# A two-layer hybrid trunk on one core: first modulation by quarters, constants on a second queue, shorter roots, and weights of the second layer split ahead

## The chip, the core and the metric

The kernel runs on one core of a Trainium2 chip. Its engines are TensorE (PE; its weight loads are listed apart as PEld), VectorE (DVE), ScalarE (ACT), GpSimd (POOL) and SyncE (SP), which issues transfers to 16 shared DMA engines. The metric is the device time of one execution in microseconds. The kernel before takes 1523.9 us (median of three runs, 1523.51 to 1525.08).

## What is computed

One inference step over 640 tokens of 1024 features: 128 prompt tokens and 512 latent tokens. Layer 0 has a mixer of gated linear attention and retention heads, layer 1 multi-head latent attention. Each layer ends in a squared-ReLU MLP with 4096 hidden features. Every sub-layer has a root-mean-square norm before and after it, and shift, scale and gate from a conditioning vector:

```python
def rms_norm(x, g=None):
    xf = x.astype(jnp.float32)
    y = xf * lax.rsqrt(jnp.mean(jnp.square(xf), axis=-1, keepdims=True) + EPS)
...
def ada_mod(cond, w_ada, b_ada):
    m = jnp.einsum('bd,de->be', jax.nn.silu(cond), w_ada) + b_ada
    return jnp.split(m[:, None, :], 6, axis=-1)

def pre_norm_mod(x, g, shift, scale):
    return rms_norm(x, g) * (1.0 + scale) + shift

def post_norm_residual(x, y, g, gate):
    return x + gate * rms_norm(y, g)

def sq_relu_mlp(h, w1, w2):
    u = jax.nn.relu(jnp.einsum('bld,df->blf', h, w1))
    return jnp.einsum('blf,fd->bld', jnp.square(u), w2)
```

The result must have float32 precision.

## The kernel before

**Tiling and precision.** The tokens are five tiles of 128 (`NT = 5`, tile 0 the prompt). A float32 product is made of three: each operand is split into a high part (`wh`, a cast by ACT) and a low part (`wl`, a difference by DVE), and `mm3` (382) multiplies high by high, low by high and high by low. `wp` is a tile that holds both parts of a narrow weight. `hT` holds the turned, modulated activations, high and low.

**Order of the work.** The program is written as generators. A list scheduler (`Weave`, 95 to 258) runs them when the program is built, with a cost table (`way`, 267) that says how long each instruction should take, and so fixes one instruction order for each engine. `_issue` (210) holds the rule for a transfer: an issue of 0.47 us, then its bytes on a modelled DMA resource. All transfers are issued by SP. A thread with a smaller priority number goes first. Rooms are `Slots`: `raw` (3) for weights as loaded, `wp` (10) for split weights, `tmp` (4), `rows` (4), and PSUM banks as `psg` (3) and `psum` (5). `weights` (478) goes through one list of weight pieces in order, takes a `raw` slot and loads; `weight_rooms` (495) takes the room for the split parts; `weight_split` (525) casts and subtracts. As one instruction is recorded from one place, every row of the profile has the line L269, and tiles tell the groups apart.

**Head.** `main` (960) loads the conditioning vectors (`cc`), `ident`, then biases and norm gains (`vec`, `post`) and `fold`. `e<-cc` on ACT starts the SiLU; `wide` holds its transpose as a stationary operand. `ada_first` (755) makes shift and scale of layer 0 by halves of 512 columns from `rada` tiles (w_ada); `FIRST_LOADS` (2312) is the order of the first loads: a for a rada load of 512 KB, x for a token tile, w for the start of the weights, c for the constants. `ada_four` (623) runs four matmuls, `ada_turned` (629) copies the row and folds it into columns. `pre_norm` (806) squares, takes the inverse root (`rsqrt`, 388), scales `x` into `xn`, turns it (`ps<-ident,xn`), makes `h` from it with shift and scale (first half all on DVE, second half all on ACT), and casts `hT`. `gemm_first` (573) multiplies it with the first 480 columns of w_in_even (`pg<-wh,hT`), half by half. `make_tables` (1496) loads the tables of the even layer late, after all first loads.

**Tails.** `out_proj` (1044) and `mlp` (1094) each have a `tail` per tile: square with a running sum (`junk,sm`), gate, `residual` (857) with an inverse root, and the next `pre_norm`. In an MLP's tail the scaled `x` is `y`. `plan` (910) lists the weight pieces: `ODD_GROUPS` are the 256 query columns and then 320 others of w_in_odd, four pieces each. The odd layer (`odd`, 1885) gives its three `psg` banks to `psum` right after the rotary query products (2042); `norm256` (1954) has one more root.

Of the kernel before, what the change touches and what calls it, by code (L numbers as in the profile page):

```python
# [94 lines left out]
class Weave:  # L95
# [114 lines left out]
    def _issue(self, eng, start):  # L210
# [13 lines left out]
        if port:  # L224
            start = max(start, self.clk.get("port", 0.0))
            self.clk["port"] = start + us
        if eng == "SP":
            th.issue = self.clk[eng] = start + 0.47
            self.clk["DMA"] = max(self.clk.get("DMA", 0.0), th.issue + 1.1) + us
            end = self.clk["DMA"] + 1.0  # L230
            th.end = end if not beside else max(th.end, end)
            if not beside:
                th.time, th.eng = max(th.time, end), eng
        else:
            self.clk[eng] = th.time = start + us
            th.eng = eng
# [24 lines left out]
class Engine:  # L261
# [5 lines left out]
    def way(self, fn, a, k):  # L267
# [6 lines left out]
        if fn == "dma_start":  # L274
            return "SP", out.shape[0] * n * 4 / 350e3, emit, False
# [56 lines left out]
class Trunk:  # L332
# [68 lines left out]


# [75 lines left out]
    def weights(self):  # L478
# [16 lines left out]
    def weight_rooms(self, loads):  # L495
        for item, load in zip(self.wlist, loads):
            if isinstance(item, Event):
                yield item
                continue
# [24 lines left out]

    def weight_split(self, raw, hr, hi, lo, held, ev, eng):
# [12 lines left out]
    def nat_units(self, w, groups, lo="vector", pair=False, rooms=[None] * 4, prio=1):  # L538
# [9 lines left out]
        return [[self.weight(src(cols, k0), [2, sum(n for _, n in cols)], lo, pair, None, rooms[k0 // 2], prio)  # L548
# [24 lines left out]
    def gemm_first(self, units, n, out, ready):  # L573

        banks = []
        for half in range(2):
            us = []
            for t in range(NT):
                yield ready[t][half]
                if half == 0:  # L580
                    banks.append((yield from self.take(self.psg, [P, 512], F32, "pg")))
                ps, hp = banks[t]
                for i in range(2):
                    if t == 0:
                        us.append((yield units[half * 2 + i]))
                    wh, wl, held = us[i]
                    for k in range(2):
                        kc = half * 4 + i * 2 + k
                        self.mm3(ps[:, :n], self.hT[0][:, t, kc], self.hT[1][:, t, kc], wh[:, k], wl[:, k],
                                 kc == 0, kc == KC - 1)  # L590
                    if t == NT - 1:
                        self.drop(*held)
                    yield
                if half:
                    self.w.set(out[t], banks[t])
# [27 lines left out]
    def ada_four(self, ps, rows, start, stop):  # L623

        self.nc.tensor.batch("matmul", [
            ((ps[32 * j:32 * j + 32], self.wide[:, kc, 2 - 2 * sec:34 - 2 * sec], raw), dict(start=start, stop=stop))
            for j, (raw, kc, sec) in enumerate(rows)], 1.4)

    def ada_turned(self, ps, n, row):

        nc = self.nc
        nc.scalar.copy(row, ps)
        yield
        for j in range(4):
# [120 lines left out]
    def ada_first(self, mod, halves, prepared, x_go, c_go):  # L755
# [5 lines left out]
        nc.vector.memset(self.wide, 0.0)  # L761

        def load():
            parts = iter([(0, sec, half, k0) for half in range(2) for k0 in range(0, KC, 2) for sec in (1, 0)])
            xs = iter(x_go)
            for kind in FIRST_LOADS:
# [4 lines left out]
                elif kind == "c":  # L771
                    w.set(c_go)
                else:
                    yield from self.ada_loads([next(parts)], self.wp, 2)
# [6 lines left out]
        for half in range(2):  # L781
            ps, hp = yield from self.bank()
            row, hw = yield from self.take(self.tmp, [P, 512], F32, "row")
            todo = [(k0, sec) for k0 in (0, 4) for sec in (1, 0)]

            for i, (k0, sec) in enumerate(todo):
                got, held = [], []
                for kc in range(k0, k0 + 4):
                    raw, hr = yield self.ada_ev[0, sec, half][kc]
                    got.append((raw, kc, sec))  # L790
                    held += hr
                self.ada_four(ps, got, i == 0, i == 3)
                self.drop(*held)
                yield
            yield self.cols_ready
            yield from self.ada_turned(ps, 4, row)
            pv = ps[:, 0:16].rearrange("p (j s c) -> p s c j", s=2, c=2)
            for sec in range(2):
                self.mod_cols(0, sec, res[sec][:, :, half * 4:half * 4 + 4], half * 4, pv[:, sec])
                w.set(halves[half][sec], res[sec])  # L800
                if half:
# [4 lines left out]
    def pre_norm(self, t, x, xn, sm, mods, ready, halves=None):  # L806
# [11 lines left out]
        evs = [Event(), Event()]  # L818

        def rest(half):  # L820
            shift, scale = halves[half] if halves else mods
            if half or not halves:
# [3 lines left out]
            for j in range(4):  # L826
                kc = half * 4 + j
# [3 lines left out]
            h, hh = yield from self.take(self.tmp, [P, 4, P], F32, "h")  # L831
            for j in range(4):
                kc = half * 4 + j
                src, bias, gain = ps[:, j * P:(j + 1) * P], sh[:, c, kc:kc + 1], sc[:, c, kc:kc + 1]
                if half:
# [5 lines left out]
            k = slice(half * 4, half * 4 + 4)  # L841
# [4 lines left out]
            w.set(evs[half])  # L846
            if halves:
                w.set(ready[t][half])

        w.spawn(rest(0))  # L850
        w.spawn(rest(1))
        yield evs[0]
        yield evs[1]
        if not halves:
            w.set(ready[t])

    def residual(self, x, yg, sm, dst=None):

        nc = self.nc
        nc.vector.tensor_scalar(sm[:, 6:7], sm[:, 4:5], sm[:, 5:6], D * EPS, op0=ALU.add, op1=ALU.add)  # L860
        yield
        yield from self.rsqrt(sm[:, 6:7], sm[:, 7:8], sm[:, 3:4], 1.0 / D)
# [19 lines left out]
    def run(self):  # L882
# [17 lines left out]
        self.ident = const("ident", [P, P])  # L900
        self.fold, self.wide = const("fold", [P, P]), const("wide", [P, KC, 34])
# [8 lines left out]
    def plan(self):  # L910
# [11 lines left out]
        self.u_in_odd = (self.nat_units(io["w_in_odd"][0], ODD_GROUPS[:1], pair=True)  # L922
                         + self.nat_units(io["w_in_odd"][0], ODD_GROUPS[1:], rooms=self.odd_rooms))
# [36 lines left out]
    def main(self):  # L960
# [7 lines left out]
        prepared, self.cols_ready = Event(), Event()  # L968
        c_go, x_go = Event(), [Event() for _ in range(NT)]
        halves = [[Event(), Event()] for _ in range(2)]  # L970
# [4 lines left out]
        ready = [[Event(), Event()] for _ in range(NT)]  # L975

        def first(t):
# [4 lines left out]
            yield from self.pre_norm(t, x, xn, sm, None, ready, halves)  # L982
            self.drop(hx, hy, hs)

        for t in range(NT):
            w.spawn(first(t), 0.0)

        load = lambda dst, src: lambda: nc.sync.dma_start(dst, src)
        k_rows = lambda nm: io[nm].rearrange("l (k p) -> (l k) p", p=P)
        arrived, arrived2 = Event(), Event()  # L990
        w.aside(load(cc[0:8], io["c_ctx"].rearrange("(k p) -> k p", p=P)),
                load(cc[8:16], io["c"].rearrange("b (k p) -> (b k) p", p=P)),
                load(self.ident, io["consts"][:, C_ID:C_ID + P]), then=lambda at: w.set(arrived, None, at))
        w.spawn(self.ada_first(mod, halves, prepared, x_go, c_go), 1.4)
        yield c_go
        w.aside(load(vec[0:96], k_rows("b_ada")), load(vec[96:112], k_rows("norm_mix_pre")),
                load(vec[112:128], k_rows("norm_mlp_pre")), load(post[0:16], k_rows("norm_mix_post")),
                load(post[16:32], k_rows("norm_mlp_post")),
                load(self.fold, io["consts"][:, C_FOLD:C_FOLD + P]), then=lambda at: w.set(arrived2, None, at))
        yield arrived  # L1000
        nc.scalar.activation(e[0:16], cc[0:16], AF.Exp, scale=-1.0)
        nc.vector.tensor_scalar(e[0:16], e[0:16], 1.0, None, op0=ALU.add)
        nc.vector.reciprocal(e[0:16], e[0:16])
        nc.vector.tensor_mul(cc[0:16], cc[0:16], e[0:16])
        ps, hp = yield from self.bank()
        nc.tensor.transpose(ps[:, 0:16], cc[0:16], self.ident[0:16, 0:16])
        nc.vector.tensor_copy(self.cT, ps[:, 0:16])
        w.set(prepared)
        yield arrived2
        yield 1.0  # L1010
        nc.tensor.transpose(ps[:, 128:256], vec, self.ident)
        nc.tensor.transpose(ps[:, 256:288], post[0:32], self.ident[0:32, 0:32])
        nc.vector.tensor_copy(self.cols, ps[:, 128:288])
        self.drop(hp, hc, he, hv, ho)
        w.set(self.cols_ready)
# [28 lines left out]
    def out_proj(self, units, oready, gate, mods, parked, gfree):  # L1044
# [6 lines left out]
        def tail(t):  # L1051
# [4 lines left out]
            for half in range(2):  # L1056
                ps, hp = yield out[half][t]
                s = slice(half * 512, half * 512 + 512)
                nc.scalar.activation(self.junk[:, 0:512], ps, AF.Square, accum_out=sm[:, 4 + half:5 + half])
                nc.vector.tensor_mul(y[:, s], ps, gr[c][:, s])  # L1060
                self.drop(hp)
# [1301 lines left out]
```

## Time and profile before

| | us |
|---|---|
| median of the runs | 1523.9 |
| the profiled execution | 1522.98 |
| its span | 1521.2 |
| PE busy | 1473.8 (97%) |
| DVE busy | 1092.6 (72%) |
| ACT busy | 651.7 (43%) |
| mean granted PE clock | 0.987 of full speed |

In the page PE's matmuls are listed apart from its weight loads, and matmuls overlap, so that a group's busy time divided by its count is the pace in a row of many and the mean of one is longer. A row of a timeline has start, duration, engine, operation, tiles and count; a bracket at its end tells how long the engine was idle before and what ended that. SPq is SP issuing. With PE at 97% the places to look at are those few in which it is not busy: the windows below give these.

### The profile page before, as it was taken

Reading aid. Unit: us, or ns where it says so; the run is one execution under the profiler, and the core shown is the slowest. Engines: PE = TensorE matmul, PEld = TensorE weight load, DVE = VectorE, ACT = ScalarE, POOL = GpSimd, SP = SyncE. Lnnn points to the kernel's source line nnn. Section 1 sums busy time; section 2 is a strip of 40 time slices with the busy share of each in tenths; the row PEclk is TensorE's granted clock in tenths of the full one; section 3 lists DMA queues with packets and bytes.
Section 4 is the critical chain, followed back from the end, with each engine's and each line's share of the span. In section 5 each row is a group of like instructions: output and inputs, shape, how many; then the busy total and the mean of one; then the engine's idle time right before and its main releaser. Section 6 shows DMA issues by size and latency. Waiting matters only on the chain.

```text
span 1521.2 us, 22996 instructions
## 1 busy us (share of the span) xinstructions
PE 1473.8 (97%) x8587; PEld 1308.4 (86%) x8587; DVE 1092.6 (72%) x2247; ACT 651.7 (43%) x1526; POOL 113.0 (7%) x133
## 2 busy tenths in 40 slices
PE   5999999999999999999997999999999999999997
PEld 2688888889899899899896989997889989988996
DVE  4464674757767877777868788885765869996776
ACT  3583533646433232233246366673654323332332
POOL 0000200101021021021010100000002000000000
PEclk8999999999999999999998999999999999999999
DMA  9546222133555444445414110104422223432332
GB/s 331 166 156 209 87 69 80 44 110 112 163 163 152 143 128 146 144 129 152 123 42 140 48 29 22 43 29 139 167 83 70 63 77 112 130 120 84 98 103 105
DMA packets 148176, 171.44 MB, mean 113 GB/s; under 512 B 12144, under 2 KB 92640, under 8 KB 148064
## 3 DMA queue, kind: packets, MB, share of 16 engines
q1 hardware_dynamic: 148064, 169.97, 36.4%
q8 instruction: 67, 1.10, 0.3%
q14 instruction: 45, 0.37, 0.1%
HBM read 161.36 MB, written 8.59 MB: 112 GB/s over the span
## 4 chain that ended last, share of the span: by engine, by line
PE 89%; DVE 4%; ACT 3%; DMA 2%; issue 1%; SPq 0%; DVEq 0%; ACTq 0%
PE p L269 55%; PE pg L269 19%; PE ps L269 13%; PE pqk L269 2%; DVE y L269 1%; PE pv L269 1%; ACT junk L269 1%; DVE sm L269 1%; DMA raw<-in_w_in_even 1%; DVE x L269 1%; DMA x<-in_x_sample 1%; DMA raw<-in_w_out_odd 1%; ACT h L269 0%; SPq L269 0%; DVE rope L269 0%
## 5 line engine op out<-in xcount | busy, mean ns | idle before, releaser
L269 PE MATMUL p<-wh,hid 128*128 128x512 f32 x1280 | 399.6, 391 | 0.0
L269 PEld LDWEIGHTS p<-wh,hid 128*128 128x128 f32 x1280 | 240.3, 188 | 49.3
L269 PE MATMUL p<-hT,wh 128*128 128x256 f32 (+1 forms) x1280 | 280.1, 310 | 0.0
L269 PE MATMUL pg<-wh,hT 128*128 128x512 f32 (+3 forms) x840 | 264.8, 389 | 0.0
L269 PE MATMUL p<-wl,hid 128*128 128x512 f32 x640 | 249.7, 390 | 0.0
L269 DVE TENSOR_TENSOR wl<-raw,wh 128x1024 fp32r<-128x1024 f32 (+3 forms) x141 | 167.9, 1195 | 73.8 <-ACT wh L269 73.4
L269 PEld LDWEIGHTS p<-hT,wh 128*128 128x128 f32 x1280 | 216.1, 190 | 0.8
L269 ACT CAST wh<-raw 128x1024 fp32r<-128x1024 f32 (+3 forms) x145 | 147.6, 1022 | 137.9 <-PE p L269 98.6
L269 PE MATMUL p<-hT,wl 128*128 128x256 f32 (+1 forms) x640 | 198.7, 310 | 0.0
L269 PEld LDWEIGHTS pg<-wh,hT 128*128 128x128 f32 x840 | 155.2, 190 | 32.3 <-issue 9.2
L269 DVE SCALAR_TENSOR_TENSOR ada<-rada,cT,ada 128x512 f32<-128x512 f32 x196 | 146.7, 778 | 0.0
L269 PE MATMUL pg<-wl,hT 128*128 128x512 f32 (+3 forms) x360 | 141.9, 394 | 0.0
L269 PEld LDWEIGHTS p<-wl,hid 128*128 128x128 f32 x640 | 120.3, 188 | 24.1
L269 DVE TENSOR_TENSOR y<-y,p 128x512 f32<-128x512 f32 x140 | 96.0, 686 | 58.1 <-PE p L269 57.3
L269 POOL TENSOR_TENSOR r<-r 128x384 f32<-128x384 f32 (+1 forms) x80 | 80.6, 1007 | 729.1 <-ACT hid L269 392.8
L269 PEld LDWEIGHTS p<-hT,wl 128*128 128x128 f32 x640 | 121.3, 190 | 0.0
L269 ACT ACTIVATE r<-p 128x384 f32<-128x384 f32 (+1 forms) x80 | 35.0, 438 | 157.1 <-PE p L269 157.1
L269 PE MATMUL p<-hT,wq 128*128 128x320 f32 x576 | 88.1, 310 | 0.0
L269 PEld LDWEIGHTS p<-hT,wq 128*128 128x128 f32 x576 | 85.5, 188 | 0.5
L269 PEld LDWEIGHTS pg<-wl,hT 128*128 128x128 f32 x360 | 68.7, 191 | 11.9 <-issue 2.5
L269 DVE TENSOR_TENSOR hid<-r,hid 128x384 fp32r<-128x384 f32 (+1 forms) x80 | 38.9, 487 | 46.4 <-POOL r L269 46.3
L269 ACT CAST wq<-tw 128x512 fp32r<-128x512 f32 x48 | 27.6, 618 | 71.0 <-DVE tw L269 61.7
(282 smaller groups left out, 2325.0 us busy)
## 6 DMA issues: line engine op xcount, KB each, us to landing
raw<-in_w_mlp SPq DMA_DIRECT2D x128, 512.0 KB, 4.1
rada<-in_w_ada SPq DMA_DIRECT2D x160, 256.0 KB, 3.2
rada<-in_w_ada SPq DMA_DIRECT2D x16, 512.0 KB, 8.7
raw<-in_w_in_even SPq DMA_DIRECT2D x16, 512.0 KB, 4.9
x<-in_x_sample SPq DMA_DIRECT2D x8, 512.0 KB, 7.0
gate<-gate SPq DMA_DIRECT2D x8, 512.0 KB, 4.5
raw<-in_w_out_even SPq DMA_DIRECT2D x8, 512.0 KB, 5.2
raw<-in_w_out_odd SPq DMA_DIRECT2D x8, 512.0 KB, 3.7
```

The costliest lines, as they stand in the source:

```text
L269: emit = lambda: real(*a, **k)
```

## The change

1. **Quarters.** `ada_first`, `pre_norm` and `gemm_first` go by quarters of 256 columns. A rada load is still 512 KB, four row blocks of 256 columns (rows of 1 KB); those of the third and fourth quarter come as two tiles each, in rooms of the even layer's pools (`early`). Of each quarter's two `h` one is DVE's and one ACT's.
2. **ACT's queue.** `vec`, `post` and `fold`, and `pos`, the first `dist` table and the ten pieces of `wf` are issued by ACT, 18 transfers. `make_tables` is cut in three parts with an event each. The scheduler's transfer rule goes by a marker and not by SP.
3. **Roots.** `root` takes sum and eps inside Ln (`bias`), the mean is made by scaling the square's input (`squares`), and the second half's sum takes the first half's as bias; the first half's sum with eps is made ahead.
4. **First MLP's tail.** `pre_norm(..., shared=True)` scales half of `x` on DVE and half on ACT.
5. **Weights ahead.** Pieces of w_in_odd have priority -1 for their splits. The third and fourth of the query columns get their split parts in two of the three `raw` slots (tiles `wr`), taken in front of their loads.
6. **Banks.** The three `psg` banks go back after the first head's projection.

The core of the diff:

```diff
+    def root(self, v, add, r, t):
+        nc = self.nc
+        nc.scalar.activation(t, v, AF.Ln, bias=add)
+        nc.scalar.activation(r, t, AF.Exp, scale=-0.5)
+        yield
+        nc.vector.scalar_tensor_tensor(t, v, add, r, op0=ALU.add, op1=ALU.mult)
+        nc.vector.scalar_tensor_tensor(t, t, -0.5, r, op0=ALU.mult, op1=ALU.mult)
+        nc.vector.scalar_tensor_tensor(r, t, 1.5, r, op0=ALU.add, op1=ALU.mult)
+
+    def squares(self, x, sm, n):
+        self.nc.scalar.activation(self.junk[:, 0:x.shape[-1]], x, AF.Square, scale=n ** -0.5, accum_out=sm)
...
+            if len(item) == 2:
+                for _ in range(item[0]):
+                    item[1].append((yield from self.take(self.raw, [P, 2, 2, 256], F32R, "wr")))
+                continue
...
+    def kept_room(self, kept):
+        t, held = kept.pop(0)
+        return t[:, 0], t[:, 1], [held]
+        yield
...
+                    q, k0, sec = part = next(parts)
+                    c0 = sec * D + q * 256
+                    if q < 2:
+                        raw, hr = yield from self.take(self.wp, [P, 4, 256], F32, "rada")
...
+                    else:
+                        rooms = yield self.early
...
+                            raw, hr = yield from self.take(min(rooms, key=lambda r: -len(r.free)), [P, 2, 256], F32, "rada")
...
-        nc.scalar.activation(self.junk, x, AF.Square, accum_out=sm[:, 0:1])
-        yield
-        nc.vector.tensor_scalar(sm[:, 1:2], sm[:, 0:1], D * EPS, None, op0=ALU.add)
-        yield
-        yield from self.rsqrt(sm[:, 1:2], sm[:, 2:3], sm[:, 3:4], 1.0 / D)
-        nc.vector.tensor_scalar(xn, x, sm[:, 2:3], None, op0=ALU.mult)
+        self.squares(x, sm[:, 0:1], D)
+        yield from self.root(sm[:, 0:1], self.eps, sm[:, 2:3], sm[:, 3:4])
+        if shared:
+            nc.vector.tensor_scalar(xn[:, 0:512], x[:, 0:512], sm[:, 2:3], None, op0=ALU.mult)
+            yield
+            nc.scalar.activation(xn[:, 512:D], x[:, 512:D], AF.Identity, scale=sm[:, 2:3])
+        else:
+            nc.vector.tensor_scalar(xn, x, sm[:, 2:3], None, op0=ALU.mult)
...
-                if half:
+                if (j if quarters else i):
                     nc.scalar.activation(h[:, j], src, AF.Identity, bias=bias, scale=gain)
...
-        nc.vector.tensor_scalar(sm[:, 6:7], sm[:, 4:5], sm[:, 5:6], D * EPS, op0=ALU.add, op1=ALU.add)
-        yield
-        yield from self.rsqrt(sm[:, 6:7], sm[:, 7:8], sm[:, 3:4], 1.0 / D)
+        yield from self.root(sm[:, 5:6], sm[:, 6:7], sm[:, 7:8], sm[:, 3:4])
...
+        self.u_in_odd = (self.nat_units(io["w_in_odd"][0], ODD_GROUPS[:1], pair=True, rooms=[None, None] + own, prio=-1)
+                         + self.nat_units(io["w_in_odd"][0], ODD_GROUPS[1:], rooms=self.odd_rooms, prio=-1))
...
+            a = nc.scalar
+            w.aside(load(vec[0:96], k_rows("b_ada"), a), load(vec[96:112], k_rows("norm_mix_pre"), a),
...
-        for _ in range(3):
-            w.give(self.psum, (yield self.psg))
...
+        def banks():
+            yield proj_ev[0]
+            for _ in range(3):
+                w.give(self.psum, (yield self.psg))
...
-FIRST_LOADS = "aacaaaxaawaxaxaaxaaxaaa"
+FIRST_LOADS = "axaaawxaxaaxaxaaaaaaaa"
```

ACT's rows from the program's first on, before (tiles have their buffer numbers; `e` is the SiLU's exponent, `junk,sm` a square and its sum):

```order
L269 ACTIVATE e_104<-cc_103 16x128
L269 ACTIVATE junk,sm_227<-x_139 128x1024
L269 ACTIVATE sm_227<-sm_227 128x1 x2
L269 ACTIVATE junk,sm_252<-x_192 128x1024
L269 COPY row_135<-ps_134 128x512
L269 CAST wh_204<-raw_145 128x960
```

and the same place on ACT with the change:

```order
L271 DMA vec_106<-in_b_ada 96x128
L271 DMA vec_106<-in_norm_mix_pre 16x128
L271 DMA vec_106<-in_norm_mlp_pre 16x128
L271 DMA post_107<-in_norm_mix_post 16x128
L271 DMA post_107<-in_norm_mlp_post 16x128
L271 DMA fold<-in_consts 128x128
L271 DMA pos<-in_consts 128x8
L271 DMA dist_159<-in_consts 128x256
L271 DMA wf_154<-in_w_gk 16x4x64 x3
L271 DMA wf_154<-in_b_gk 1x4x64 x2
L271 ACTIVATE e_105<-cc_104 16x128
L271 COPY row_275<-ps_237 128x256
```

The second set of `wf` rows stands behind the first, and `e` and everything else on ACT stand behind all of them.

SP's rows with the change in the middle of the head, where the loads of the third quarter end and those of the fourth begin:

```order
L271 DMA rada_273<-in_w_ada 128x2x256
L271 DMA rada_274<-in_w_ada 128x2x256
L271 DMA raw_323<-in_w_in_even 128x2x32
L271 DMA raw_323<-in_w_in_even 128x2x448
L271 DMA raw_372<-in_w_in_even 128x2x256
L271 DMA rada_280<-in_w_ada 128x2x256
L271 DMA rada_423<-in_w_ada 128x2x256
L271 DMA rada_436<-in_w_ada 128x2x256
```

Three weight loads, which need a `raw` slot, stand ahead of the last quarter's; before, the last rada loads of shift and scale stood here, and the weights of the same columns around them.

PE's rows behind the first MLP's last products, before (`wp_7263` and `wp_7266` are the first two weight pieces of the query columns, `wp_7478` the third; `pg_7562` is the first tile's product; `y_3653` and `y_3655` are the third and fourth tile's scaled rows, turned into `hT`):

```order
L269 MATMUL pg_7562<-wp_7266,hT_91 128x256 x2
L269 MATMUL pg_7562<-wp_7266,hT_92 128x256
L269 MATMUL ps_7590<-ident,y_3653 128x128
L269 MATMUL ps_7591<-ident,y_3653 128x128
...
L269 MATMUL ps_7639<-ident,y_3655 128x128
L269 MATMUL ps_7640<-ident,y_3655 128x128
...
L269 MATMUL pg_7562<-wp_7478,hT_91 128x256 x2
L269 MATMUL pg_7562<-wp_7478,hT_92 128x256
```

and with the change (`wr` are the kept pieces, third and fourth; `pg_7718` is the second tile's product, `y_3741` and `y_3743` the third and fourth tile's rows):

```order
L271 MATMUL pg_7656<-wp_7353,hT_91 128x256 x2
L271 MATMUL pg_7656<-wp_7353,hT_92 128x256
L271 MATMUL pg_7656<-wr_7309,hT_91 128x256
L271 MATMUL ps_7671<-ident,y_3741 128x128
...
L271 MATMUL pg_7656<-wr_7364,hT_91 128x256
L271 MATMUL pg_7718<-wp_7350,hT_91 128x256 x2
L271 MATMUL pg_7718<-wr_7309,hT_91 128x256 x2
L271 MATMUL pg_7718<-wr_7364,hT_91 128x256 x2
L271 MATMUL ps_7816<-ident,y_3743 128x128
L271 MATMUL ps_7817<-ident,y_3743 128x128
```

All four pieces of the first tile and of the second now stand ahead of the fourth tile's transposes.

More of the change, by code (lines that the diff above doesn't have):

```diff
@@ L546, in src @@
             return parts
-        return [[self.weight(src(cols, k0), [2, sum(n for _, n in cols)], lo, pair, None, rooms[k0 // 2], prio)
+        return [[self.weight(src(cols, k0), [2, sum(n for _, n in cols)], lo, pair or sum(n for _, n in cols) <= 256, None, rooms[k0 // 2], prio)
                  for k0 in range(0, KC, 2)] for cols in groups]
@@ L780, in ada_first @@
         nc.vector.tensor_copy(self.wide[:, :, 2:4], self.cT.rearrange("p (c k) -> p k c", c=2))
-        for half in range(2):
+        for q in range(4):
             ps, hp = yield from self.bank()
-            row, hw = yield from self.take(self.tmp, [P, 512], F32, "row")
-            todo = [(k0, sec) for k0 in (0, 4) for sec in (1, 0)]
             for i, (k0, sec) in enumerate(todo):
[L787 to L792, printed above, removed]
+                got, held = yield evs[q, k0, sec]
+                self.ada_four(ps, [(got[k], k0 + k, sec) for k in range(4)], i == 0, i == 3)
                 self.drop(*held)
@@ L825, in rest @@
             ps, hp = yield from self.bank()
-            for j in range(4):
-                kc = half * 4 + j
+            m = KC // n
+            for j in range(m):
+                kc = i * m + j
                 nc.tensor.transpose(ps[:, j * P:(j + 1) * P], xn[:, kc * P:(kc + 1) * P], self.ident)
@@ L845, in rest @@
             self.drop(hh)
[L846 to L854, printed above, removed]
+            w.set(evs[i])
+            if quarters:
+                w.set(ready[t][i])
+        for i in range(n):
+            w.spawn(rest(i))
+        for ev in evs:
+            yield ev
+        if not quarters:
             w.set(ready[t])
@@ L921, in plan @@
         self.odd_rooms = [Event() for _ in range(4)]
-        self.u_in_odd = (self.nat_units(io["w_in_odd"][0], ODD_GROUPS[:1], pair=True)
-                         + self.nat_units(io["w_in_odd"][0], ODD_GROUPS[1:], rooms=self.odd_rooms))
+        own = [Event() for _ in range(2)]
+        kept = []
+        for ev in own:
+            ev.at, ev.value = 0.0, lambda: self.kept_room(kept)
+        self.u_in_odd = (self.nat_units(io["w_in_odd"][0], ODD_GROUPS[:1], pair=True, rooms=[None, None] + own, prio=-1)
+                         + self.nat_units(io["w_in_odd"][0], ODD_GROUPS[1:], rooms=self.odd_rooms, prio=-1))
+        first = next(i for i, x in enumerate(self.wlist) if isinstance(x, tuple) and len(x) == 8 and x[6] is own[0])
+        self.wlist.insert(first, (2, kept))
         wq = io["w_q_b"][0].rearrange("(k p) (h c) -> p k h c", p=P, h=HC)
@@ L974, in main @@
         self.running = [Event(), Event()]
-        ready = [[Event(), Event()] for _ in range(NT)]
+        ready = [[Event() for _ in range(4)] for _ in range(NT)]
         def first(t):
@@ L981, in first @@
             sm, hs = yield from self.small()
-            yield from self.pre_norm(t, x, xn, sm, None, ready, halves)
+            yield from self.pre_norm(t, x, xn, sm, None, ready, quarters)
             self.drop(hx, hy, hs)
@@ L994, in main @@
[L994 to L1012, printed above, removed]
```

226 lines of the change are left out of this document (133 added, 93 removed).

## The prediction

> **What bounds the kernel now.** I read the page first, then the windows by stage, then the timelines of the stages in which TensorE (PE) is not full. The page:
>
> ```profile
> span 1521.2 us, 22996 instructions
> PE 1473.8 (97%) x8587; PEld 1308.4 (86%) x8587; DVE 1092.6 (72%) x2247; ACT 651.7 (43%) x1526; POOL 113.0 (7%) x133
> ```
>
> The run around this span took 1522.98 us, 0.9 under the median of 1523.9; my sum is made against 1523.0. PE is the bound. So an edit can win only where PE stands still or runs at a low granted clock. The windows (PE busy, PEld, DVE, ACT, POOL; then PEclk, DMA share, GB/s) show where that is:
>
> ```profile
> 0.00:20.00 20.00, 7.69 (x27) 1.57 (x27) 3.84 (x12) 3.15 (x6) 0.93 (x6) 1.00 0.83 276
> 20.00:34.00 14.00, 8.67 (x39) 3.83 (x38) 9.23 (x30) 8.03 (x16) 0.00 (x0) 0.62 1.05 394
> 34.00:60.00 26.00, 22.23 (x117) 16.31 (x117) 12.41 (x30) 12.65 (x29) 0.00 (x0) 0.89 0.57 189
> 60.00:100.00 40.00, 39.77 (x265) 30.87 (x264) 19.87 (x48) 30.80 (x85) 1.58 (x3) 0.95 0.49 150
> 800.00:830.00 30.00, 19.88 (x107) 17.32 (x106) 26.36 (x71) 20.21 (x59) 0.00 (x0) 0.77 0.40 130
> 860.00:905.00 45.00, 41.59 (x272) 38.21 (x271) 37.05 (x116) 24.68 (x78) 4.25 (x9) 1.00 0.07 18
> 1490.00:1521.00 31.00, 21.96 (x97) 17.84 (x96) 22.88 (x50) 9.16 (x30) 0.00 (x0) 0.90 0.23 85
> ```
>
> PE lacks 12.3 + 5.3 + 3.8 = 21.4 us in the first 60 (the head), 10.1 in 800 to 830 (first MLP's end into the odd layer), 3.4 in 860 to 905, 9.0 at the end; 60 to 100 is full. These four places are also those that the edits touch. The head on PE:
>
> ```profile
> 8.64 3.63 PE L269 MATMUL ps<-rada,wide 128*32 128x512 f32 x12
> 31.79 1.94 PE L269 MATMUL ps<-rada,wide 128*32 128x512 f32 x8
> 33.66 0.77 PE L269 MATMUL pg<-wh,hT 128*128 128x480 f32 x1
> 58.95 1.97 PE L269 MATMUL ps<-ident,xn 128*128 128x128 f32 x8 [3.77 <-ACT h L269]
> 62.72 0.77 PE L269 MATMUL pg<-wh,hT 128*128 128x480 f32 x1
> 82.37 0.28 PE L269 MATMUL pg<-wh,hT 128*128 128x256 f32 x1
> ```
>
> The first 480-column product (pg) starts at 33.66, its second half waits for ScalarE's `h` and goes on at 62.72, and the next column group starts at 82.37. Up to there both programs hold nearly the same PE work; whatever the change wins in the head is how much earlier than 82.37 this point comes.
>
> **The head: quarters and ACT's queue.** The loads, and what ACT and SP do there:
>
> ```profile
> GB/s 0 47 194 401 243 292 212 270 318 378 401 393 400 400 401 384 382 392 397 396 397 394 393 383 384 379 385 382 335 188 31 0 0 18 309 47 12 182 75 36
> 2.92 0.47 SPq L269 DMA_DIRECT2D vec<-in_b_ada  x1
> 5.29 0.42 SPq L269 DMA_DIRECT2D fold<-in_consts  x1
> 12.82 0.37 SPq L269 DMA_DIRECT2D raw<-in_w_in_even  x1
> 14.96 0.37 SPq L269 DMA_DIRECT2D rada<-in_w_ada  x1
> 2.72 0.31 ACT L269 ACTIVATE e<-cc 16x128 f32<-16x128 f32 x1 [0.71 <-DMA cc<-in_c]
> 22.91 0.58 ACT L269 COPY row<-ps 128x512 f32<-128x512 f32 x1
> 55.99 3.60 ACT L269 ACTIVATE h<-ps,mod,mod 128x128 f32<-128x128 f32 x10
> ```
>
> Slices of the first row are 1.5 us: 3.5 MB are in by 15 us, then the engines move about 390 GB/s up to 43. Before, a half of shift and scale (4 MB) must be there before its row is copied (22.91), and between the copy and the first pg lie 10.8 us of folds, mods, `h`, casts and late x tiles. With quarters 2 MB do, and they and the first x are in by about 13 us.
>
> *What is late next:* `e`. In the change 18 DMAs (six for vec, post and fold, then pos, dist and ten wf) stand on ACT ahead of it. At 0.42 to 0.47 each (vec and fold rows) they take about 8 us: `e` at 2.72 + 8 = 10.8. But from 12.82 on SP issues only every 2.1 us (12.82 to 14.96) with an issue of 0.37, so outstanding DMAs are limited, and if ACT's share that limit, the last wf wait for SP's transfers: five such steps add up to 7 us, `e` at 18. I take 14, the middle. Then `wide` 2.6 us later (e's exponent, four small DVE steps, transpose, copy), 16 matmuls in four batches at 1 us (12 took 3.63): row at about 21; a row, two folds, mods, two `h` on two engines, cast and difference of half the former width, about 4.5: first pg at **25.5 instead of 33.7**.
>
> From there to 82.37 PE took 48.7 us before, of which 3.8 waited for `h` and about 1 in smaller gaps: 44 of work. Of shift and scale and transposes more is left now: about 26 matmuls of the size of the 31.79 row (0.24 each at that clock, near 0.13 at a full one) and eight transposes, 4.5 us together. 25.5 + 48.5 = 74; with a wait of 0 to 3 us for the third or fourth quarter and a slow clock left out in one place (the serial `h` of 55.99 are shared between DVE and ACT now) I take 72.4: **−10**. Bounds: −15 (`e` at 10.8, no wait) and −2. SP loses 18 issues of 0.45, 8 us, but with engines full from 15 to 43 this brings no byte earlier; cost 0. 1 KB rows in place of 2 KB: of the page's loads of 256 KB
>
> ```profile
> rada<-in_w_ada SPq DMA_DIRECT2D x160, 256.0 KB, 3.2
> raw<-in_w_in_even SPq DMA_DIRECT2D x4, 256.0 KB, 2.8
> ```
>
> the first has 2 KB rows and the second 1 KB rows; no price shows. I take 0, with the 13% between them, 2.7 us on 8.4 MB at 390 GB/s, to either side (in the bounds above).
>
> **First MLP into the odd layer.** PE and DVE before:
>
> ```profile
> 808.49 1.59 PE L269 MATMUL pg<-wp,hT 128*128 128x256 f32 x12
> 812.43 1.06 PE L269 MATMUL ps<-ident,y 128*128 128x128 f32 x8 [2.35 <-DVE y L269]
> 817.63 1.97 PE L269 MATMUL ps<-ident,y 128*128 128x128 f32 x8 [3.80 <-DVE y L269]
> 822.60 1.44 PE L269 MATMUL pg<-wp,hT 128*128 128x256 f32 x5 [2.79 <-DVE wp L269]
> 825.21 1.97 PE L269 MATMUL ps<-ident,y 128*128 128x128 f32 x8 [1.17 <-DVE y L269]
> 826.83 6.44 PE L269 MATMUL pg<-wp,hT 128*128 128x256 f32 x43
> 813.40 0.27 DVE L269 TENSOR_SCALAR sm<-sm 128x1 f32<-128x1 f32 x2
> 810.31 1.23 ACT L269 CAST wp<-raw 128x512 fp32r<-128x512 f32 x2
> 821.87 0.68 DVE L269 TENSOR_TENSOR wp<-raw,wp 128x512 fp32r<-128x512 f32 x1
> 824.40 0.75 DVE L269 TENSOR_SCALAR y<-x,sm 128x1024 f32<-128x1024 f32 x1
> ```
>
> From 808.49 to 826.83 are 18.3 us, in which PE has 18 pg (0.15 each by the 43 in 6.44), 24 transposes (0.13 by 1.06 for 8) and little else: 6.4 us at a full clock, **12 us lost**. The chain is DVE's: it is busy 26.4 of 30. The change splits the third and fourth weight pair ahead (kept in two raw slots) and so puts some 54 pg, 54 × 0.15 = 8.1 us, ahead of the last tile's transposes; it takes a 0.68 split, about five 0.14 additions and half of five 0.75 scalings (to ACT) from DVE's chain, 3.2 us. Then: 13 pg to 810.5, a wait for the third tile's `y` until about 811.7, 48 rows at a clock first low, to 820.5; the fourth tile's `y` (before 817.6) is there, 24 pg more to 825, and the last `y` is ready near 822. Left lost: 1.5 of waits and 2.2 of clock. **−8.3**; bounds −12 (nothing lost) and −3 (below).
>
> The clock is weighed here: in 20 to 34 it is granted at 0.62 and in 800 to 830 at 0.77, though no single wait quoted above is longer than 3.8 us. The Trainium skill, "TensorE: Matmul & The Clock Gate", Part 1, says that the clock halves only after a free-running window of about 3.4 us has been idle. By that rule the waits of 1.5 us left in this stage would leave the clock full and the term would be −10.5, where by the 0.77 row it is −8.3; I go by the row.
>
> **The rest.** Three banks come back to psum only after the first head's projection: they serve the products at 860 to 905 longer, where PE lacks 3.4. I take −0.7, between −3 (all of it) and +2 (scores wait for a bank, at the size of the 2.35 wait). The shorter root shows at the end, where nothing covers it:
>
> ```profile
> 1514.12 0.19 ACT L269 ACTIVATION_READ_ACCUMULATOR junk<-y 128x1 f32 x1
> 1514.95 0.21 DVE L269 TENSOR_SCALAR sm<-sm 128x1 f32<-128x1 f32 x1
> 1515.19 0.44 ACT L269 ACTIVATE sm<-sm 128x1 f32<-128x1 f32 x2 [0.88 <-DVE sm L269]
> 1515.66 0.22 DVE L269 SCALAR_TENSOR_TENSOR sm<-sm 128x1 f32<-128x1 f32 x1 [0.51 <-ACT sm L269]
> ```
>
> The sum of 1514.95 and its wait of 0.88 on ACT go; the three DVE steps that follow stay three: −0.8, or −0.3 if DVE, busy with a product until the sum, is still what ends last. I take −0.6. At the two ends of out_proj, both covered in part by PE work, −0.8 together (0 to −2). Elsewhere PE is full and roots, masks and tables are hidden by it: 0.
>
> **Sum:** −10 − 8.3 − 0.7 − 0.6 − 0.8 = −20.4; 1523.0 − 20.4 = **1502.6**.
>
> **Rivals.**
> *A. The head moves, its end does not.* All bytes of shift and scale still pass the same engines, full to 43; the last quarter comes when the last half came. PE's order is fixed, so a late quarter stops the rows behind it. For it: before, the second half went on (62.72) 19 us after the engines fell off at 43; a last quarter needs at least 8 of these (fold, mods, ten `h` of 0.36 shared, casts), and the first pg rows run slow. Against it: the next quarter's 30 products (6.6 us) wait ready. The head then gives −2 to −5: 1508 to 1511, say **1509**. The Trainium skill says as much in "DMA: Bandwidth & Descriptors", section "Issuing engines are not separate DMA queues": the transfers of all issuers interleave on the same 16 engines, and a second issuer saves sequencer time only. By that the 18 moved issues win nothing in the head; the full slices between 15 and 43 agree.
>
> *B. One raw slot.* With two of three raw slots kept, the 320-column loads of the next group go through one: landing 3.1, cast 0.6 (810.31), split 0.7 (821.87), issue 0.4, 4.8 each, four of them 19 us, beside 5 × 24 × 0.15 = 18 us of PE work. If they begin after 808 they end near 827, and PE waits there instead. Term −3 in place of −8.3: **1508**.
>
> ```profile
> raw<-in_w_in_even SPq DMA_DIRECT2D x2, 320.0 KB, 3.1
> ```
>
> *C. Slower: SP's queue stands in the head.* The last quarter's loads wait for rooms that the third quarter's matmuls free, in PE's order; behind them on SP stand the weights of the following groups and the tables. Each us that the last of them lands after about 55 (72.4 less 6.6 of its products, 8 of its chain, 3 of slack) is a us of PE. The gain is gone when it lands at about 75, and at 80 the kernel needs **1528**. Speaks for it: rooms are given back only behind products; against: before the last landed near 43, and 30 us are long beside waits of 2 to 4.
>
> *D. It does not do what it says:* the tail stays DVE's chain with new work on ACT, `e` waits to 18 and the quarters win nothing: −3 of small terms, **1520** to 1523.
>
> **How the numbers follow.** Forecast (1497 to 1507) 0.55; A or B alone (1507 to 1512) 0.22; A and B together (1512 to 1518) 0.07; more than forecast (under 1497: both upper bounds at work) 0.07; D 0.04; C 0.05. About 0.2%, 3 us, is what a measurement of this kernel can tell from no change. Faster 0.91, within 0.03 (half of D and a little), slower 0.06. A, B and the forecast hold 0.84; with a little of each end left out and the unknown prices of the 1 KB rows, `e` and the banks (together about 5 us) added to the sums, the range for 8 in 10 goes from 1492 to 1516.
>
> **What would show it.** Right: first pg near 25 to 27, the first 256-column pg near 72, PE without a wait over 2 us between 812 and 830 of before's count, Ln straight behind the last accumulator read. Wrong: `e` past 18, PE waiting over 5 us for `rada` or `h` after 40 (A), waits on `raw` or `wp` of 320 columns (B), SP standing on a rada load past 55 (C). A stage behind the head that is not full any more would show that the gain is given back to weight loads, which nothing in the full row of 60 to 100 suggests.

## The result

The changed kernel takes 1512.16 us (median of four runs, 1510.94 to 1513.31) against 1523.7 us of the kernel before in the same sessions; the ratio is 0.9925, 95% interval 0.9912 to 0.9937. That is 11.5 us less, where 20.4 were forecast; the time lies inside the range of 1492 to 1516.

The page of the changed kernel, first two lines, and its windows (PE busy, PEld, DVE, ACT, POOL; then PEclk, DMA share, GB/s), answering to those of before:

```profile
span 1508.8 us, 23115 instructions
PE 1468.6 (97%) x8651; PEld 1304.4 (86%) x8651; DVE 1085.8 (72%) x2234; ACT 659.4 (44%) x1543; POOL 114.5 (8%) x133
...
0.00:20.00 20.00, 1.54 (x11) 0.92 (x15) 2.94 (x12) 3.13 (x6) 0.93 (x6) 1.00 0.78 240
20.00:34.00 14.00, 11.25 (x69) 4.26 (x59) 5.77 (x17) 7.29 (x17) 0.00 (x0) 1.00 1.06 368
34.00:60.00 26.00, 21.68 (x158) 13.38 (x155) 17.66 (x52) 16.82 (x42) 0.00 (x0) 1.00 0.72 234
...
800.00:830.00 30.00, 26.68 (x178) 24.43 (x177) 26.83 (x75) 23.38 (x68) 0.00 (x0) 0.94 0.39 124
1480.00:1509.00 29.00, 20.96 (x93) 17.04 (x91) 22.07 (x50) 9.51 (x30) 0.00 (x0) 0.90 0.24 91
```

The stage from 800 to 830 is fuller by 6.8 us of PE and its clock is 0.94 instead of 0.77. The head is not: PE does 1.5 us in the first 20, where it did 7.7 before. The starts of a few PE rows in the timelines say where the 12.4 us of the span come from ("480" is the first column group, "MLP" the first of its second products, "odd" the first product of the odd layer, "key" and "value" its first key and last value product, "last" the last product of all):

| kernel | first 480 | last 480 | MLP | odd | key | value | last | span |
|---|---|---|---|---|---|---|---|---|
| before | 33.66 | 81.91 | 387.26 | 808.49 | 867.58 | 1040.22 | 1511.58 | 1521.2 |
| changed | 30.57 | 82.76 | 387.73 | 807.66 | 859.21 | 1028.75 | 1500.57 | 1508.8 |

Stage by stage: +0.5 to the MLP, −1.3 in it, **−7.5** from odd to key (59.09 to 51.55), **−3.1** from key to value (172.64 to 169.54), +0.5 from value to last, **−1.4** at the end (9.6 to 8.2). The head, for which −10 was forecast, gave nothing. The stages are of one profiled execution each; in the head two executions of one order differ by up to 1.4 us (shown below).

Its first rows on PE, with the first of the next column group:

```profile
18.19 0.28 PE L271 MATMUL ps<-ident,cc 16*128 16x16 f32 x1 [18.19 <-DMA wf<-in_w_gk]
19.39 1.94 PE L271 MATMUL ps<-rada,wide 128*32 128x256 f32 x16
30.57 0.77 PE L271 MATMUL pg<-wh,hT 128*128 128x480 f32 x1
83.19 0.36 PE L271 MATMUL pg<-wp,hT 128*128 128x256 f32 x1
```

ACT's timeline at the same time:

```profile
4.89 0.44 ACTq L271 DMA_DIRECT2D dist<-in_consts  x1
5.43 2.69 ACTq L271 DMA_DIRECT2D wf<-in_w_gk  x3
8.16 3.00 ACTq L271 DMA_DIRECT2D wf<-in_b_gk  x2
11.20 3.48 ACTq L271 DMA_DIRECT2D wf<-in_w_gk  x3
14.92 1.31 ACTq L271 DMA_DIRECT2D wf<-in_b_gk  x2
16.29 0.31 ACT L271 ACTIVATE e<-cc 16x128 f32<-16x128 f32 x1 [14.27 <-DMA wf<-in_w_gk]
```

`e`, with which shift and scale begin, starts at 16.29 and not at 2.72. The ten wf issues take ACT 10.8 us: 6.8 in the issues themselves (0.57 to 1.16 each; on SP in the kernel before the same ten took 6.2) and 4.0 in waits for earlier transfers. SP's waits in the first 60 us show the other side of it (engine, waited for: us, times, longest):

```profile
SPq L271 <- DMA wf<-in_w_gk: 3.7, 3, 2.2
SPq L271 <- DMA wf<-in_b_gk: 3.5, 1, 3.5
```

SP's own issues wait 7.2 us for landings of ACT's small transfers. The trace records the reason: each transfer of SP or ACT completes on one of eight semaphores (101 to 108), which the two queues use in turn, and an issue waits until the transfer that had its semaphore before has landed.

### The profile page after: what moved, and what is told of

It is laid out like the page before. It is cut to its first block, busy times and chain, and to the rows that moved or that the text cites. A ratio compares the mean times of both kernels' runs of the same rounds, so it can differ in the third digit from the quotient of the medians.

```text
span 1508.8 us, 23115 instructions
## 1 busy us (share of the span) xinstructions
PE 1468.6 (97%) x8651; PEld 1304.4 (86%) x8651; DVE 1085.8 (72%) x2234; ACT 659.4 (44%) x1543; POOL 114.5 (8%) x133
## 4 chain that ended last, share of the span: by engine, by line
PE 93%; DVE 3%; ACT 2%; DMA 1%; issue 0%; SPq 0%; DVEq 0%; ACTq 0%
PE p L271 57%; PE pg L271 21%; PE ps L271 13%; PE pqk L271 2%; PE pv L271 1%; DMA rada<-in_w_ada 1%; DVE sm L271 0%; DVE y L271 0%; DVE rope L271 0%; DMA x<-in_x_prompt 0%; ACT junk L271 0%; DVE x L271 0%; DMA wf<-in_w_gk 0%; ACT sm L271 0%; ACT hT L271 0%
## 5 line engine op out<-in xcount | busy, mean ns | idle before, releaser
L271 PE MATMUL pg<-wh,hT 128*128 128x512 f32 (+2 forms) x760 | 245.9, 399 | 1.2 <-ACT hT L271 0.9
L271 DVE TENSOR_TENSOR wl<-raw,wh 128x1024 fp32r<-128x1024 f32 (+2 forms) x137 | 165.3, 1209 | 76.0 <-ACT wh L271 70.8
L271 ACT CAST wh<-raw 128x1024 fp32r<-128x1024 f32 (+2 forms) x141 | 144.8, 1033 | 132.1 <-PE p L271 88.4
L271 PEld LDWEIGHTS pg<-wh,hT 128*128 128x128 f32 x760 | 140.0, 189 | 31.2 <-issue 4.7
L271 PE MATMUL pg<-wl,hT 128*128 128x512 f32 (+2 forms) x320 | 130.5, 408 | 0.0
L271 PEld LDWEIGHTS pg<-wl,hT 128*128 128x128 f32 x320 | 60.7, 190 | 15.2 <-issue 3.9
```

Source lines behind the costliest of these rows:

```text
L271: emit = lambda: real(*a, **k)
```

## The experiments

**The tables off ACT's queue.** The changed kernel, with only the twelve table transfers put back behind SP's first loads.

```diff
         def make_tables():
-            a = nc.scalar
+            yield self.loaded
+            yield 2.0
+            a = nc.sync
```

> The changed kernel with the twelve table transfers (pos, dist, ten wf) back on SP's queue behind the first loads; vec, post and fold stay on ACT's. Theory 1 (the tables on ACT hold e and SP's loads, and this eats the gain of the quarters): e near 5 us instead of 16.3, first 480-column product near 23 to 25 instead of 30.6, the first MLP's products begin 6 to 9 us earlier than 387.7, time 1503 to 1506. Theory 2 (the head's end is set by SP standing for raw slots ahead of the last quarter's loads, whatever e does): e and the first product come earlier as well, but the first MLP still begins within 2 us of 387.7, time 1510 to 1514.

Measured: **1499.94 us** (1499.48 to 1501.0), ratio to before 0.9843 (0.9827 to 0.986). That is 12.2 us under the changed kernel. ACT and PE:

```profile
3.82 0.31 ACT L271 ACTIVATE e<-cc 16x128 f32<-16x128 f32 x1 [1.80 <-DMA ident<-in_consts]
...
14.59 0.37 ACT L271 COPY row<-ps 128x256 f32<-128x256 f32 x1 [5.33 <-PE ps L271]
14.87 1.06 ACT L271 ACTIVATE junk<-x 128x1024 bf16<-128x1024 f32 x1
```

```profile
21.47 0.77 PE L271 MATMUL pg<-wh,hT 128*128 128x480 f32 x1
```

The first 480-column product is at 21.47, the last at 68.10 (81.91 before), the MLP at 375.72: 12.0 us earlier than with the tables on ACT, and all of it lasts to the end. Theory 1 stands, with more than it expected (12 us at the MLP for 6 to 9); theory 2 falls.

**Is it `e`, or are SP's loads held?** The kernel of the last run, with idle work on ACT ahead of `e`, and no transfer moved. The squares of a constant have no use.

```diff
+            nc.gpsimd.memset(self.gate[0], 0.0)
+            nc.scalar.batch("activation", [((self.junk, self.gate[0], AF.Square), {}) for _ in range(12)], 0.1)
             yield arrived
             nc.scalar.activation(e[0:16], cc[0:16], AF.Exp, scale=-1.0)
```

> The kernel of tables_on_sp (1499.9 us) with twelve squares of a constant tile put on ACT ahead of e, about 12.5 us of ACT's time, whose results nobody uses; every transfer is where it was in that run, and the orders of all engines are the same. Theory a (the delay of e alone costs the 12 us): e near 16, first 480-column product near 31, time 1509 to 1513, like the changed kernel. Theory b (what costs is that the small tables take turns with SP's loads and hold these): e near 16, but shift and scale are in SBUF when e comes and PE catches up, time 1502 to 1506.

Measured: 1510.7 us (1509.52 to 1512.28). ACT, and SP's later issues, of this run:

```profile
3.73 13.02 ACT L271 ACTIVATE junk<-gate 128x1024 bf16<-128x1024 f32 x12 [1.72 <-DMA ident<-in_consts]
16.66 0.29 ACT L271 ACTIVATE e<-cc 16x128 f32<-16x128 f32 x1
```

```profile
32.33 7.99 SPq L271 DMA_DIRECT2D raw<-in_w_in_even  x3
40.37 7.99 SPq L271 DMA_DIRECT2D rada<-in_w_ada  x10
```

Apart from the squares and the fill of their tile the traces of the two runs have the same instructions in the same order on every engine. With `e`, and what stands behind it on ACT, 12.8 us late and nothing else done, 10.8 of the 12.2 us are there: theory a. The rest is not clear of the noise (ratios 0.9912, 0.9898 to 0.9927, and 0.9925, 0.9912 to 0.9937). SP stands for `raw` slots at 32.33 here (8 us for three issues; 1.7 in the run before, 5.9 in the changed kernel). As no transfer was moved, that is a result of the late products, which free the slots. With half the dose:

> Like e_late, with six idle squares instead of twelve: e comes about 6.3 us later than in tables_on_sp (3.8), near 10. If everything behind e is one chain from the first us on, the cost is in proportion: 1504.5 to 1506. If loads still had to land for the first few us, a part of the delay is hidden: 1500 to 1503.

Measured: 1503.24 us (1502.82 to 1504.29), `e` at 10.21:

```profile
10.21 0.29 ACT L271 ACTIVATE e<-cc 16x128 f32<-16x128 f32 x1
```

The first 6.4 us of delay cost 3.3, the next 6.4 cost 7.5. In tables_on_sp PE still waits for loads of shift and scale ahead of its first 480-column product:

```profile
9.12 1.08 PE L271 MATMUL ps<-rada,wide 128*32 128x256 f32 x8 [0.91 <-DMA rada<-in_w_ada]
```

There are five such waits, 2.6 us in all; in e_half there is none. So 2.6 us of the delay were covered by loads: the first product is 3.8 us later in e_half (25.28) and another 6.4 in e_late (31.73), a us for each us of `e`. Neither expectation was met; the truth lies between.

**Other queues.** The twelve tables by GpSimd:

```diff
         def make_tables():
 
-            a = nc.scalar
+            a = nc.gpsimd
```

> The changed kernel with the twelve table transfers issued by GpSimd, early, instead of ACT; vec, post and fold on ACT. If only what stands behind them on ACT counts: like tables_on_sp, 1498 to 1502. If early small transfers hold SP's loads whichever engine issues them: 1503 to 1510, with SP's rada issues late.

Measured: 1499.75 us (1498.81 to 1499.93), like tables_on_sp. GpSimd has only a few fills to do in the head, ahead of these issues, and so nobody waits behind them. Its transfers also have eight semaphores of their own in the trace, so that this run takes away the issues on ACT and the shared semaphores together; e_late is the run that parts them. With the other six on SP too:

```diff
-            a = nc.scalar
+            a = nc.sync
             w.aside(load(vec[0:96], k_rows("b_ada"), a), load(vec[96:112], k_rows("norm_mix_pre"), a),
```

> The kernel of tables_on_sp with vec, post and fold on SP as well, so that ACT issues no transfer in the head. If the second queue for these six is a gain: 1502 to 1504, as SP's first loads come 2 to 3 us later. If it is worth nothing: 1499 to 1501.

Measured: **1498.8 us** (1498.54 to 1499.33), ratio 0.9835 (0.9818 to 0.9851), the lowest median here, but not clear of the noise from tables_on_sp (0.9827 to 0.986). So no gain of ACT's queue shows with these six either. `e` is at 8.92 here, and the time is not longer for that, unlike in e_half:

```profile
8.92 0.29 ACT L271 ACTIVATE e<-cc 16x128 f32<-16x128 f32 x1
```

Here the scheduler knew of the later `e` and put the first tile's square ahead of it and those of the next tiles ahead of the first row copy on ACT; in tables_on_sp the second tile's square (14.87) stands behind that copy (14.59). The first 480-column product is late here too (23.95, against 21.47), but the last is not (68.21, against 68.10): what is lost up to the first is made up behind it, in 44.3 us from first to last instead of 46.6. That the order is what does it is argued from the rows, not tried.

**The other parts alone, on the kernel before.** Roots, shared scaling, weights ahead and banks, with the old head:

> The kernel before, with its head by halves and its constants on SP, and only the shorter roots, the shared scaling in the first MLP's tail, the weights ahead and the late return of the banks. If the new head is worth nothing (both traces have the first MLP's products begin at 387 to 388): 1511 to 1513, like the changed kernel. If the new head is a gain that something else in the changed kernel takes back later: 1515 or more. If the new head is a loss: under 1510.

Measured: 1514.79 us (1513.35 to 1515.14), ratio 0.9938 (0.9917 to 0.9958). These parts bring 8.5 us; the time lies between the first two expectations. The new head without the tables on ACT brings 14.9 more (1499.94); with them, 2.6. It is not 0, since with the old head these parts let the MLP begin at 391.35, 4.1 us later than before. Of this the roots alone, in the run below, show 3.1, and the banks alone show 1.4, though every engine has there the order of before up to 867.9: so much of it can be what two executions differ by. Why the rest is lost was not looked into. The three edits, each alone:

> The kernel before with the weights ahead alone (kept raw slots and priority -1). Theory: PE stood still because it had too little split weight to work on, so this alone brings most of the 7.5 us between 808 and 868: 1516 to 1518. Rival: VectorE's tail chain sets it, and the shorter roots and shared scaling are what moved it: 1521 to 1524.

> The kernel before with the three banks given back after the first head's projection, alone. Theory: the 3.1 us gained between 868 and 1040 are from this: 1520 to 1521.5. Rival: they come from the order that the scheduler found behind an earlier start, and this alone does nothing: 1523 to 1525.

> The kernel before with the shorter roots and the shared scaling alone. The end of the last tail should be 1.2 to 1.4 us shorter (9.6 us from the last product's start to the end of the span before, 8.2 in the changed kernel). For the odd layer between 868 and 1040: if the 3 us won there are from the roots, this shows 2 us or more of them and the time is 1519 to 1521; if they need the weights ahead and the banks together, it shows under 1 us and the time is 1521.5 to 1523.

Measured: weights ahead 1516.26 us (0.9948, 0.9929 to 0.9966); banks 1523.85 (1.0005, 0.9995 to 1.0014); roots and shared scaling 1523.02 (0.9995, 0.9983 to 1.0006). Their edits are the lines of the diff above that carry them (the entries of two in the weight list with `wr` and `kept_room`; the generator `banks`; `root`, `squares` and `shared`). PE's waits between the MLP and the odd layer, for before, for weights ahead alone, and for the changed kernel:

```profile
PE ps L269 <- DVE y L269: 7.3, 3, 3.8
PE pg L269 <- DVE wp L269: 2.8, 1, 2.8
```

```profile
PE ps L269 <- DVE sm L269: 2.3, 1, 2.3
PE pg L269 <- ACT wp L269: 0.5, 1, 0.5
```

```profile
PE ps L271 <- DVE ql L271: 1.4, 2, 1.2
PE pg L271 <- DVE wp L271: 1.3, 1, 1.3
PE ps L271 <- DVE y L271: 0.8, 1, 0.8
```

The weights ahead carry the stage: alone they take 6.4 us from odd to key (809.31 to 861.99), the roots alone 2.9 (811.39 to 867.57), both 7.5 in the changed kernel. But the roots alone do not make the kernel faster: their head is later (first 480-column product at 35.27, MLP at 390.39, 3.1 us behind before), which eats it in this execution; up to 1.4 us of that can be chance, as above. Nor do they give the 3 us of the odd layer, which is 173.9 us from key to value in that run. Weights ahead alone have 172.4 there and the banks alone 173.2, against 172.6 before; all these parts together, with the old head, have 170.2. So the 3 us come from the parts together, and not from the new head.

**Taken away one at a time.** From the kernel of tables_on_sp, without the late banks and without the weights ahead:

```diff
+        for _ in range(3):
+            w.give(self.psum, (yield self.psg))
...
-        for g in (projections, all_values, banks, scores, turns, outputs, finish, out_rooms):
+        for g in (projections, all_values, scores, turns, outputs, finish, out_rooms):
```

> The kernel of tables_on_sp (1499.9) with the three banks given back at once, as before. If the late return of the banks does win in the odd layer once the weights stand ready (alone it won nothing): 1501.5 to 1504, and the time from the first key product (pqk) to the last value product (pt,v) grows from 170.3 back towards 172.6. If it is worth nothing here too: 1499 to 1501.

```diff
-        self.u_in_odd = (self.nat_units(io["w_in_odd"][0], ODD_GROUPS[:1], pair=True, rooms=[None, None] + own, prio=-1)
-                         + self.nat_units(io["w_in_odd"][0], ODD_GROUPS[1:], rooms=self.odd_rooms, prio=-1))
+        self.u_in_odd = (self.nat_units(io["w_in_odd"][0], ODD_GROUPS[:1], pair=True)
+                         + self.nat_units(io["w_in_odd"][0], ODD_GROUPS[1:], rooms=self.odd_rooms))
```

> The kernel of tables_on_sp without the weights ahead (no kept raw slots, priority as before). If they carry the stage between the MLP and the odd layer here as they did alone (6.4 of 7.5 us): 1505.5 to 1508. If the shorter tail carries the stage once it is there: 1501 to 1503.

Measured: without banks 1509.03 us (1506.64 to 1509.72), 9.1 more; without weights ahead 1509.59 (1507.81 to 1510.47), 9.7 more. Both are above their expectations. But without the banks all engines have the order of tables_on_sp up to 847.3, and 3.0 of the 9.1 us are lost ahead of that point (1.0 up to the MLP, 2.0 from odd to key, with the clock at half for 6.8 us there instead of 3.4): in the profiled execution 6.1 us lie behind it. Of these 6.0 are in the odd layer: key to value is 176.4 us against 170.3, and PE waits there again, early in it. Its three longest kinds of wait:

```profile
PE pv L271 <- DVE rope L271: 1.6, 1, 1.6
PE ps L271 <- DVE qs L271: 1.4, 1, 1.4
PE pv L271 <- DVE qn L271: 0.6, 1, 0.6
```

Against these stands one kind of wait in about the same stretch of tables_on_sp:

```profile
PE ps L271 <- DVE qs L271: 1.4, 2, 1.1
```

Without the weights ahead 1.3 us are lost up to the MLP, where the edit has not begun, 1.1 in it, 4.4 from odd to key and 2.9 from key to value (173.2 us): the edit is worth 4.4 us in its own stage here, and not 6.4. The prices of these parts do not add: alone the two are worth 7.0 and 0, last taken away 9.7 and 9.1 (8.4 and 6.1 without what is lost ahead of the edit). What the banks need beside them is open. It is not the weights alone: only_ahead has these with the banks given back at once, and its 172.4 us from key to value are no more than before's. A kernel with weights and roots, but without the banks, on the old head was not run; nor was tables_on_sp without both.

## Why the prediction was right in sign and wrong in its largest term

**The head (−10 forecast, +0.5 measured): the step on `e`.** "What is late next: `e`" named the mechanism, and the forecast even had the reason, ACT's issues sharing a limit with SP's. The size was wrong three times. `e` was put at 14, "the middle"; it came at 16.29. The sum took 0.44 us for each issue from the rows of vec and fold, where a wf issue takes 0.62 in the middle, and did so on SP in the kernel before: ten of them are 1.8 us more, and 4.0 of waits come on top. From `e` to the first product were counted 11.5 us; they are 14.3. From there to the end of the group 46.9 were counted, and from 30.57 to the first 256-column product at 83.19 are 52.6. The first and the second add up to 5.1 us, the third is 5.7.

The count from `e` to the first product had only the first tile in it. The fixed orders have two. The first tile's part is in `hT` at 28.03; on PE the second tile's transposes and eight matmuls for a later quarter stand ahead of the first product (30.57), and the transposes wait for that tile's `xn` on DVE:

```profile
28.13 0.75 DVE L271 TENSOR_SCALAR xn<-x,sm 128x1024 f32<-128x1024 f32 x1
28.94 0.69 PE L271 MATMUL ps<-ident,xn 128*128 128x128 f32 x2 [2.26 <-DVE xn L271]
29.56 1.08 PE L271 MATMUL ps<-rada,wide 128*32 128x256 f32 x8
```

`xn` needs that tile's square and root. On ACT the square stands behind the first row copy, and that behind the matmuls of shift and scale, so behind `e`. The third miss is that from first to last 480-column product the changed kernel takes 52.2 us. In e_late, with `e` as late and the tables on SP from 48 to 57 us, it is 47.1; in tables_on_pool, where the tables come early but not through ACT, 48.0. So the early tables by themselves go with some 1.4 us (46.6 in tables_on_sp); what makes the rest was not parted, and most of it is made up by the MLP (1.2 us between the changed kernel and e_late).

The quarters do win: with `e` at 3.82 they bring 13.8 us at the last 480-column product and 11.5 at the MLP. But for the `e` that it assumed the forecast put them too high. In e_half, with `e` at 10.21, the first 256-column product is at 72.29, 10.1 us ahead of before, where the bound with `e` at 10.8 was −15; between e_half and e_late (79.05 with `e` at 16.66) an `e` of 14 would give some −6, an estimate by interpolation, where −10 was taken.

**The range.** That the time lies inside it is owed to its width. 1512.2 falls into the bracket of 1512 to 1518, which had 0.07 for A and B together, and neither is what happened. The half of D that is about the head, `e` waits and the quarters win nothing, is; its half about the tail is not, and D had 0.04 in all.

**Rivals A and C.** The last quarter of A did not decide: PE of the changed kernel waits for ACT's row copies and casts between 20 and 84 us, and never for a rada load:

```profile
PE ps L271 <- ACT row L271: 3.5, 3, 1.8
PE pg L271 <- ACT hT L271: 0.9, 2, 0.6
```

From `e` at 10.21 on the head's end moves with `e` (6.8 us for 6.4 between e_half and e_late). But the part of A that the moved issues win nothing is borne out (all_on_sp). The Trainium skill, "DMA: Bandwidth & Descriptors", section "Issuing engines are not separate DMA queues", says that a second issuer saves its sequencer's time only; the runs agree, and here ACT's own time was the loss. C's mechanism, SP standing for rooms, is there (5.9 us at 33.42), but it grows with a late `e` alone (1.7, 3.6 and 8.0 us in tables_on_sp, e_half and e_late) and so follows from the late products.

**MLP into odd layer (−8.3 forecast, −7.5 measured).** Right, by its own mechanism: before, PE had four waits of 10.1 us in all; now there are four of 3.5 us, none over 1.3. Rival B, one raw slot, shows as a wait of 1.3 us on `wp`, not as the bound. On the clock the windows of the changed kernel decide:

```profile
815.00:820.00 5.00, 2.25 (x14) 1.53 (x13) 4.49 (x15) 4.97 (x19) 0.00 (x0) 1.00 0.57 181
820.00:825.00 5.00, 4.42 (x25) 4.39 (x26) 4.80 (x17) 3.23 (x8) 0.00 (x0) 0.66 0.45 164
825.00:830.00 5.00, 5.00 (x44) 5.00 (x43) 3.72 (x11) 3.82 (x11) 0.00 (x0) 1.00 0.54 175
```

No wait there is over 1.3 us, and the clock still falls to 0.66 in the mean of 820 to 825, after a stretch in which PE was busy 2.25 of 5 us. By the rule of the Trainium skill, "TensorE: Matmul & The Clock Gate", Part 1, that a window of about 3.4 us has to be idle first, as the prediction read it, this term would have been −10.5. The trace does not agree with that reading: in the 3.4 us ahead of the fall (817.2 to 820.6) PE was busy for 1.25. The "only" is the prediction's and not the page's. The row of before was the better guide.

**Banks (−0.7 forecast, −3.1 measured between key and value).** Within the bounds of −3 to +2 but for 0.1, and at the wrong end: the forecast priced the edit in the stage as it was. no_banks shows that its worth, 6.0 us in this stage there, comes with the other edits.

**The end (−0.6 forecast, −1.4 measured).** The root of the last half now begins right behind the accumulator's read. From that read to the last scaling of `x`:

```profile
1502.82 0.19 ACT L271 ACTIVATION_READ_ACCUMULATOR junk<-y 128x1 f32 x1
1503.04 0.53 ACT L271 ACTIVATE sm<-sm 128x1 f32<-128x1 f32 x2
1503.65 0.60 DVE L271 SCALAR_TENSOR_TENSOR sm<-sm 128x1 f32<-128x1 f32 x3
1504.29 1.41 DVE L271 SCALAR_TENSOR_TENSOR x<-y,sm,x 128x512 f32<-128x512 f32 x2
```

Before, these were 2.18 us (1514.12 to 1516.30), and now they are 1.47: the forecast's −0.6 was right, by the sum and its wait of 0.88 us that are gone; the three DVE steps take 0.64 as before. Of the rest, 0.3 lie between the last product and the read (2.55 to 2.25 in every kernel with the new root; why was not looked into), and 0.3 behind the scaling, where kernels with this tail range from 4.5 to 4.9 us. **Out_proj's ends** (−0.8 forecast) show nothing: value to last, which holds one of them, is 0.5 us longer. The three stages that fell, odd to key, key to value and the end, make −12.0 of −12.4, and the term that carried half the forecast is not among them.

## What to carry to other kernels

A transfer issued by an engine that also computes is an instruction in that engine's order: if its issue has to wait, everything behind it waits. Look at what stands behind it first; twelve small table loads ahead of one 0.31 us activation cost 12 us of 1500, and on an idle queue no cost shows. Price an edit also with its neighbours in place: two edits that alone were worth 7 and 0 us cost 9.7 and 9.1 when they were taken away last. And where the order of two programs is the same up to an edit, what differs ahead of it is not the edit's.

## What was not expected of the hardware

Issues on two queues held each other: ten wf issues of 16 KB and less held ACT for 10.8 us while SP's 512 KB loads were under way, 4.0 of it in waits, and SP waited 7.2 us for their landings. By the trace's records the thing shared is the program's set of eight semaphores, which the transfers of SP and ACT use in turn in every run here, with SP alone too. Whether the queues share anything else is not shown.

And the granted clock in the windows is 1.00 for the first 34 us of the changed kernel, although three of its 480-column products start 0.40 us apart there (31.77 to 32.56) and 0.22 from 35.74 on. In the kernel before the same pace (0.40 from 34.22 to 36.62) has 0.50 beside it. The changed kernel's trace has its first change of the clock on record at 35.53. So where a trace has none on record yet, the pace of the products is the better measure.
